# One gate/up block of a SwiGLU layer computed by Strassen's scheme in the Winograd form

## The chip, the cores and the metric

The kernel runs on one NeuronCore of a Trainium2 chip, alone. The metric is the device time of one execution in microseconds (us); lower is better. A core has five instruction streams: TensorE (PE; its weight loads are shown apart as PEld), VectorE (DVE), ScalarE (ACT), GpSimd (POOL) and SyncE (SP), the last used here only to issue DMAs. PE writes to PSUM, eight banks of 2 KB a partition; all else lives in SBUF.

## The reference, cut to what matters

The kernel computes one layer of a hybrid decoder for 256 tokens, all in float32. The change lies in the last two steps.

```python
D_MODEL = 1024; SEQ = 256
D_FF = -(-8 * D_MODEL // (3 * 256)) * 256          # 2816

def layer(x, ...):
    h = rms_norm(x, ln1_g)
    x = x + (sigmoid(g_a) * attention(h) + sigmoid(g_b) * ssm(h)) @ w_out
    h2 = rms_norm(x, ln2_g)
    x = x + (silu(h2 @ w_gate) * (h2 @ w_up)) @ w_down
    h3 = rms_norm(x, ln3_g)
    return x + (p @ w_ple_proj) * sigmoid(h3 @ w_ple_gate)
```

## The kernel before

**Splitting float32.** TensorE multiplies at its fast rate in a rounded format, so each float32 operand `a` is kept as `ah` (rounded) and `al = a - ah`, and each product takes three matmuls, `ah*wh + ah*wl + al*wh`, that add up in one PSUM bank. Activations are split once; weights on their way in. A weight tile is 128 rows x 2 k-tiles x 512 columns (512 KB). SP issues its load to `raw` (4 buffers), ACT rounds it to `wh` (5 buffers), and DVE subtracts to get `wl` (5 buffers): `split_w`, whose subtraction is L377 and whose rounding goes through the helper `act` at L254. Every matmul goes through the helper `mm` at L275.

**Panels.** A `Panel` is 256 tokens x 512 output columns in two PSUM banks (tiles named g), one for each half of the tokens. Its inner dimension of 1024 is eight k-tiles; `next_chunk()` gives four of them (two weight tiles), and a half panel is the 24 matmuls of 128x512 that these four feed: 4 k-tiles x 3 x 2 token halves.

**SwiGLU.** The 2816 columns of gate and of up are taken as five blocks of 512 and one of 256. A block is a gate panel and an up panel, four half panels or 96 matmuls. `Gated.gate` computes silu for each token half: ACT takes Sigmoid of the bank scaled by the row's `rstd2`, and DVE multiplies it by the scaled bank (L1509). `Gated.up` multiplies by the up bank (L1518), a DVE transpose turns 32x32 squares (L1527), and `send` moves the 16 pieces of 32 KB to their place with 16 DMAs issued on SP's queue (L1537). `split`, a task that waits until its due time, rounds the moved rows on ACT and subtracts on DVE (L1549); they are the operands of the down-projection, whose two panels of 22 k-tiles follow the gate/up blocks. Then `Residual` adds (L1432) and normalises, and `final` (L1600 to L1605) applies the last gate.

**What sets the order.** Each engine runs its own instructions in the order in which they were issued when the kernel was built, and waits on semaphores for the others. The order is made in the builder: `fill.spawn` registers a task, a generator that yields the model time at which it is due; `fill.step()` after each k-tile advances that time, and due tasks are issued there. `LAG`, and numbers such as 26000.0 in `split`, are such due times in model nanoseconds. `prio` ranks instructions for the scheduler, and `follow` holds one behind another. So a number in a table decides where in an engine's stream an instruction stands, and the hardware then takes it in that place.

Of the kernel before, what the change touches and what calls it, by code (L numbers as in the profile page):

```python
# [13 lines left out]
ALU = mybir.AluOpType  # L14
# [48 lines left out]
]  # L63
NFF = 11

NORMED = 5


def by_rows():
# [63 lines left out]
    "m": [11900, 6200],  # L133
    "res": [5337, 5987],
    "m.moved": [11625, 22875],
    "r.moved": [15000],
}
# [52 lines left out]
def tile_layer(ctx: ExitStack, tc: tile.TileContext, head, xk, pt, vec, w_dt, w_big, w_dn2, w_pp, out):  # L190
# [170 lines left out]

    def w_tiles():
        return (sb.tile([P, 2, 512], F32, tag="raw", bufs=RAW, name=nm("raw")),
                sb.tile([P, 2, 512], F32R, tag="wh", bufs=WH, name=nm("wh")),
                sb.tile([P, 2, 512], F32R, tag="wl", bufs=WL, name=nm("wl")))

# [1052 lines left out]
    class Residual:  # L1419
# [7 lines left out]
        def take(self, n, pan):  # L1427
# [51 lines left out]
    for n in range(2):  # L1479
# [15 lines left out]
    ff = []  # L1495

    class Gated:

        def __init__(self, w):
            self.w, self.f = w, []  # L1500

        def gate(self, pan, c):

            with prio("ev"):
                for tt, ps in enumerate(pan.ps):
                    r = rstd2[:, tt : tt + 1]
                    f = s2([self.w])
                    act(f, ps[:, c], AF.Sigmoid, scale=r)
                    stt(f, ps[:, c], r, f, op0=ALU.mult, op1=ALU.mult)  # L1509
                    self.f.append(f)  # L1510
# [20 lines left out]
        def send(self, turned):  # L1531
            n = self.both.shape[3]
            moved = s4([4, 2 * n])
            with prio("ev"):
                for a in range(4):
                    for b in range(4):
                        nc.sync.dma_start(  # L1537
                            moved[32 * b : 32 * b + 32, a], self.both[32 * a : 32 * a + 32, b].rearrange("p t n -> p (t n)"))
            fill.spawn(self.split(moved.rearrange("p a (x j) -> p x a j", j=32)), 0)

        def split(self, moved):

            yield fill.now + (26000.0 if self.w > 256 else 26500.0)
            n = self.w // P
            with prio("ev"):
# [25 lines left out]
    gated = Gated(512)  # L1571
    gated.gate(pans[0], WHOLE)
    gated.up(pans[1], WHOLE)
    for n in range(1, NFF // 2):
        gated = Gated(512)
        gated.gate(pans[2] if n == 1 else whole(), WHOLE)
        gated.up(whole(), WHOLE)
    pan = Panel()
    for k in (0, 4):
        pan.add(next_chunk(), h2[k : k + 4], last=k == 4)  # L1580
    gated = Gated(256)
    gated.gate(pan, HALVES[0])
    gated.up(pan, HALVES[1])

    res3 = Residual(xin, V_G3, rstd3, False)
    for n in range(2):
        pan = Panel()
        for c in range(4):
            ch = next_chunk()
            fill.drain(lambda: len(ff) >= 4 * c + 4)  # L1590
            pan.add(ch, ff[4 * c : 4 * c + 4], last=False)
        ch = next_chunk() + load(w_dn2[n], 2)
        fill.drain(lambda: len(ff) == 22)
# [16 lines left out]
def _layout(i):  # L1610
# [79 lines left out]
```

## Time and profile before

| | |
|---|---|
| three runs | 574.41, 575.56, 576.28 us; median 575.56 |
| the profiled execution | 574.76 us |
| its span, first to last instruction | 572.8 us |
| granted TensorE clock | 1.00 throughout |
| gate/up and down-projection | about 310 to 553 us of the span |
| GpSimd busy | 88.0 us (15%) |

Times come from the profile of one execution. "Busy" is the time in which an engine ran an instruction; groups of instructions are given by source line, engine, operation and shape, with the mean duration of one; "idle before" is the time in which the engine waited ahead of them, with what ended it. The chain that ended last is followed back from the last instruction; where it stays on one engine, that engine was never waiting. Rows on which the argument rests stand with the prediction.

### The profile page before, as it was taken

To read this page: it belongs to the slowest core of one execution; us is meant where nothing else is said; L and a number is where in the kernel's file an instruction comes from. 1 tells how busy PE (TensorE), PEld (TensorE's weight loads), DVE (VectorE), ACT (ScalarE), POOL (GpSimd) and SP (SyncE) were. 2 spreads that over 40 slices of the span, in tenths; PEclk is the share of its full clock that TensorE was granted. 3 is DMA by queue.
4 is the path that set the end of the run, shared out by engine and by line. 5 is a ranking of instruction groups with operands and counts; after the bars stand their busy time and mean duration, and the time that the engine had idled before them with its cause. 6 is when DMAs were issued, how large, how long until landed. Compare 5 with 4: busy or idle time off the path is not lost.

```text
span 572.8 us, 8553 instructions
## 1 busy us (share of the span) xinstructions
PE 567.3 (99%) x2971; PEld 476.0 (83%) x2971; DVE 444.5 (78%) x702; ACT 339.7 (59%) x532; POOL 88.0 (15%) x127
## 2 busy tenths in 40 slices
PE   9999999999999999999999999999999999999996
PEld 8887898988888888888887888888888888888885
DVE  6678899989999988898695976766767767556565
ACT  6855567676779579748574454646355445444452
POOL 2011223000533403211320200300000000002020
PEclk9999999999999999999999999999999999999999
DMA  8875698656476756757655785575677666657652
GB/s 317 325 265 175 222 266 238 208 153 180 156 191 185 208 177 173 257 162 249 186 168 190 267 287 194 167 273 184 197 238 242 210 214 233 219 190 256 196 173 73
DMA packets 43802, 121.22 MB, mean 212 GB/s; under 512 B 6384, under 2 KB 14608, under 8 KB 43760
## 3 DMA queue, kind: packets, MB, share of 16 engines
q1 hardware_dynamic: 39040, 107.71, 57.0%
q0 software_dynamic: 4144, 12.32, 8.6%
q10 hardware_dynamic: 576, 0.66, 0.4%
q8 instruction: 23, 0.38, 0.3%
q14 instruction: 19, 0.16, 0.1%
HBM read 111.28 MB, written 6.44 MB: 205 GB/s over the span
## 4 chain that ended last, share of the span: by engine, by line
PE 98%; DMA 1%; DVE 0%; ACT 0%; issue 0%
PE g L275 88%; PE pb L275 8%; PE pb L297 2%; DMA raw<-in_head 1%; ACT s L254 0%; DVE s L1603 0%; DVE s L1604 0%; DVE wh L373 0%
## 5 line engine op out<-in xcount | busy, mean ns | idle before, releaser
L275 PE MATMUL g<-wh,s 128*128 128x512 f32 (+1 forms) x1220 | 381.8, 390 | 0.1
L254 ACT ACTIVATE wh<-raw 128x1024 fp32r<-128x1024 f32 (+2 forms) x192 | 198.9, 1039 | 159.5 <-PE g L275 125.0
L377 DVE TENSOR_TENSOR wl<-raw,wh 128x1024 fp32r<-128x1024 f32 (+2 forms) x188 | 223.6, 1194 | 81.4 <-ACT wh L254 73.3
L275 PEld LDWEIGHTS g<-wh,s 128*128 128x128 f32 x1220 | 228.7, 189 | 47.5 <-issue 0.5
L275 PE MATMUL g<-wl,s 128*128 128x512 f32 (+1 forms) x610 | 235.6, 388 | 0.0
L275 PEld LDWEIGHTS g<-wl,s 128*128 128x128 f32 x610 | 114.6, 188 | 23.2 <-issue 0.4
L275 PE MATMUL g<-s,wh 128*128 128x512 f32 (+1 forms) x320 | 90.3, 353 | 0.0
L275 PE MATMUL g<-s,wl 128*128 128x256 f32 x256 | 69.2, 283 | 0.0
L275 PEld LDWEIGHTS g<-s,wh 128*128 128x128 f32 x320 | 54.8, 190 | 6.8 <-DVE s L1392 0.3
L275 PEld LDWEIGHTS g<-s,wl 128*128 128x128 f32 x256 | 48.5, 189 | 2.0 <-issue 0.2
L254 ACT ACTIVATE s<-s 128x512 f32<-128x512 f32 (+4 forms) x45 | 34.9, 786 | 17.6 <-DVE s L1432 5.6
L749 POOL DMA_DIRECT2D turn_d<-s x16 | 12.6, 788 | 194.9 <-DVE s L739 194.5
L275 PEld LDWEIGHTS pb<-s,s 128*64 128x64 f32 (+2 forms) x336 | 23.9, 158 | 5.8 <-issue 2.4
L275 PE MATMUL pb<-s,s 128*64 128x128 f32 (+5 forms) x336 | 28.7, 294 | 0.0
L254 ACT ACTIVATE s<-pb 128x512 f32<-128x512 f32 (+3 forms) x45 | 20.3, 481 | 13.7 <-PE pb L275 8.4
L254 ACT ACTIVATE s<-s,vecs 128x256 f32<-128x256 f32 (+1 forms) x48 | 23.3, 536 | 6.3 <-DMA s<-turn_d 5.3
L653 DVE SCALAR_TENSOR_TENSOR s<-s,vecs,s 128x255 f32<-128x255 f32 (+2 forms) x60 | 26.4, 478 | 0.0
L759 POOL DMA_DIRECT2D s<-turn_d x40 | 22.5, 595 | 25.3 <-DMA turn_d<-s 10.3
L886 POOL TENSOR_SCALAR_AFFINE_SELECT rr<-a_h 128x512 fp32r<-128x512 f32 x16 | 16.8, 1134 | 37.9 <-PE pb L275 21.6
L254 ACT ACTIVATE s<-s,tiny 128x128 f32<-128x128 f32 (+1 forms) x44 | 18.7, 444 | 5.9 <-DVE tiny L1086 5.9
L254 ACT ACTIVATE s<-g 128x256 f32<-128x256 f32 (+1 forms) x44 | 20.0, 472 | 1.3 <-PE g L275 1.3
L794 POOL TENSOR_TENSOR tiny<-tiny,mhalf 128x8 f32<-128x8 f32 x8 | 13.2, 1649 | 42.0 <-DVE tiny L792 41.6
(153 smaller groups left out, 382.0 us busy)
## 6 DMA issues: line engine op xcount, KB each, us to landing
raw<-in_w_big SPq DMA_DIRECT2D x176, 512.0 KB
turn_d<-s POOLq DMA_DIRECT2D x14, 256.0 KB, 4.7
s<-turn_d POOLq DMA_DIRECT2D x28, 128.0 KB, 4.9
wl<-in_w_big POOLq DMA_DIRECT2D x5, 512.0 KB, 8.0
s<-s SPq DMA_DIRECT2D x80, 32.0 KB
raw<-in_head SPq DMA_DIRECT2D x4, 512.0 KB
s<-in_xk SPq DMA_DIRECT2D x4, 512.0 KB
raw<-in_head SPq DMA_DIRECT2D x6, 256.0 KB
```

What stands on the lines that cost most here:

```text
L254: return nc.scalar.activation(o, i, f, **kw)
L275: ins = nc.tensor.matmul(o, lhsT, rhs, start=start, stop=stop).ins
L297: queue(nc.tensor.transpose(o, i, ident[: i.shape[0], : i.shape[0]]).ins, main)
L377: low = nc.vector.tensor_sub(wl, raw, wh.bitcast(F32))
L653: stt(cc[j][:, sft:], pu[:, j, : T - sft], cw[j][3 - sft], cc[j][:, sft:], op0=ALU.mult, op1=ALU.add)
L749: nc.gpsimd.dma_start(d[:, :, at : at + t_.shape[2]].rearrange("b p n -> p b n"), t_)
L759: by[via[b % len(via)]].dma_start(o[32 * b : 32 * b + 32], d[b].rearrange("(a i) n -> i a n", i=32))
L794: nc.gpsimd.tensor_tensor(f, ms, mhalf, op=ALU.pow)
L886: nc.gpsimd.affine_select(r, bcast(a_h[:, c, h0 : h0 + 4].bitcast(F32), P), pattern=[[0, 4], [1, P]], compare_op=ALU.is_ge, fill=0.0, base ...
```

## The change

The fourth of the five 512 blocks (`wino_block()` is 3, columns 1536 to 2047 of gate and of up) is computed as a product of 2x2 block matrices: the two token halves are the rows, the two halves of the inner dimension the middle, and gate and up the columns. Winograd's form of Strassen's scheme needs seven block products in place of eight. Each has 12 matmuls of 128x512 (4 k-tiles x 3) and a PSUM bank of its own (tiles named pb), so that the block takes 84 matmuls.

- **Weight sums.** `b11`, `b21` are gate's two K halves, `b12`, `b22` up's. A chain `q` in two SBUF tiles holds b11 for P1, has b12 added for P5, b22 for P6 and b21 for P4; a chain `r` holds b22 for P3 and has b12 added for P7; P2 takes b21 as it is. Each product has two tiles of 512 KB loaded and splits them as any other weight tile: 14 tiles where the block had 8. Of the eight additions of 128x1024, six are on VectorE and the two of P4 on GpSimd.
- **Activation sums.** `wino_rows` builds them on GpSimd from the split rows (one token half rescaled by the ratio of the two `rstd2`, which one more float32 matmul, `pr`, spreads over the partitions), and splits three of them with ACT and DVE.
- **Order.** `whole()` calls `gw.step()` ahead of the half panels numbered 1, 2, 4, 5, 6, 7 and 8 (`WINO_AT`), so one product runs before each: P1, P2, P5, P3, P6, P7, P4. The other blocks keep their order.
- **SiLU.** ACT computes Silu in one instruction; DVE's multiplication at L1509 is gone. In `final`, Sigmoid becomes Tanh of half the argument; `hrstd3` is that half, and `pj` is halved when it is evicted.
- **Moves.** The 16 DMAs of each block are issued from GpSimd's queue, four at a time in steps of `GAP`, and no longer from SP's. The due times of `split` and two rows of `LAG` are set anew.

```diff
+GAP = 1049
+WINO_AT = (1, 2, 4, 5, 6, 7, 8)
+SUMS = {('P2', 0), ('P3', 0), ('P3', 1), ('P5', 0), ('P5', 1), ('P6', 0), ('P6', 1), ('P7', 0), ('P7', 1)}
+ROWS = [18485, 28895, 2039, 6021, 1453, 0]
+SPLIT_AT = [58803, 53214]
...
-    "res": [5337, 5987],
+    "res": [4481, 1462],
...
-    "r.moved": [15000],
+    "r.moved": [19998],
...
+                        if not self.normed:
+                            nc.gpsimd.tensor_scalar(hrstd3[:, tt : tt + 1], self.dst[:, tt : tt + 1], 0.5, None, op0=ALU.mult)
...
-                copy = nc.vector.tensor_copy(pj[n][:, tt], pan.ps[tt])
+                copy = nc.vector.tensor_scalar(pj[n][:, tt], pan.ps[tt], 0.5, None, op0=ALU.mult)
...
+    def wino_rows():
+        yield fill.now + ROWS[0]
...
+        with prio("bg"):
...
+            pr = pb([P])
+            mm(pr, ones, rd, True, True)
+            prs = s2([P])
+            act(prs, pr)
+            a1, a2 = s4([2, 4, P]), s4([2, 4, P])
+            for h in range(2):
+                for k in range(4):
+                    hi, lo = (x.bitcast(F32) for x in res2.acts[h][k][:2])
+                    ptt(a2[:, h, k], hi[:, P:], lo[:, P:], op=ALU.add)
+                ptt(a2[:, h], a2[:, h], prs.unsqueeze(1).to_broadcast([P, 4, P]), op=ALU.mult)
...
+            ptt(a1[:, 0], a2[:, 0], a1[:, 0], op=ALU.subtract)
+            ptt(q, a1[:, 0], a2[:, 1], op=ALU.subtract)
+            ptt(a2[:, 0], a2[:, 0], a2[:, 1], op=ALU.subtract)
+            ptt(a1[:, 1], a1[:, 1], q, op=ALU.add)
+        for n, (a, ps) in enumerate(((a2, ("P5", "P4")), (a1, ("P7", "P3")), (q, ("P6",)))):
+            yield fill.now + ROWS[2 + n]
...
+                follow(act(h, a).ins, fill.cast)
+                nc.vector.tensor_sub(l, a, h.bitcast(F32))
...
+    class Wino:
+        TAKES = {"P1": ("q", "b11"), "P5": ("q", "b12"), "P6": ("q", "b22"), "P4": ("q", "b21"),
+                 "P3": ("r", "b22"), "P7": ("r", "b12"), "P2": (None, "b21")}
...
+                        if (chain, i) not in self.held:
+                            self.held[chain, i] = s4([2, 512])
+                            nc.sync.dma_start(self.held[chain, i], src)
+                        else:
+                            more = sb.tile([P, 2, 512], F32, tag="raw", bufs=RAW, name=nm("raw"))
+                            nc.sync.dma_start(more, src)
+                            on = nc.vector if (p, i) in SUMS else nc.gpsimd
+                            on.tensor_tensor(self.held[chain, i], self.held[chain, i], more, op=ALU.add)
+                        tiles = (self.held[chain, i], *w_tiles(1))
+                    fill.cast = split_w(tiles).ins
...
+        def product(self, p, ps=None, begin=True, end=True):
+            parts = self.load(p)
+            fill.drain(lambda: len(self.acts.get(p, ())) == len(parts))
...
+            for k, ((wh, wl), (ah, al)) in enumerate(zip(parts, self.acts[p])):
+                with prio("mm"):
+                    mm(ps, ah, wh, begin and k == 0, False, main=True)
+                    mm(ps, ah, wl, False, False, main=True)
+                    mm(ps, al, wh, False, end and k == len(parts) - 1, main=True)
+                fill.step()
...
-                    act(f, ps[:, c], AF.Sigmoid, scale=r)
-                    stt(f, ps[:, c], r, f, op0=ALU.mult, op1=ALU.mult)
+                    act(f, ps[:, c], AF.Silu, scale=r)
...
+        def moves(self, both):
+            n = both.shape[3]
             moved = s4([4, 2 * n])
-            with prio("ev"):
-                for a in range(4):
+            for a in range(4):
+                with prio("ev"):
                     for b in range(4):
-                        nc.sync.dma_start(
-                            moved[32 * b : 32 * b + 32, a], self.both[32 * a : 32 * a + 32, b].rearrange("p t n -> p (t n)"))
+                        follow(nc.gpsimd.dma_start(
+                            moved[32 * b : 32 * b + 32, a], both[32 * a : 32 * a + 32, b].rearrange("p t n -> p (t n)")).ins, fill.last)
+                yield fill.now + GAP
...
-            yield fill.now + (26000.0 if self.w > 256 else 26500.0)
+            yield fill.now + SPLIT_AT[self.w == 256] - 4 * GAP
...
+    class GatedWino(Gated):
...
+            p1 = product("P1")
+                act(v1, p1, scale=r)
+            p2 = product("P2")
+                stt(c11, p2, r, v1, op0=ALU.mult, op1=ALU.add)
+                act(f1, c11, AF.Silu)
+            p5 = product("P5")
+            p3 = product("P3")
+            p6 = product("P6")
+                stt(v1, p6, r, v1, op0=ALU.mult, op1=ALU.add)
+                stt(c12, p5, r, v1, op0=ALU.mult, op1=ALU.subtract)
+                stt(c12, p3, r, c12, op0=ALU.mult, op1=ALU.add)
+                nc.vector.tensor_mul(f1, f1, c12)
+            p7 = product("P7")
+                stt(v1, p7, r, v1, op0=ALU.mult, op1=ALU.subtract)
+                stt(c22, p5, r, v1, op0=ALU.mult, op1=ALU.add)
+                turned = [self.turn(f1, 0)]
+            p4 = product("P4")
+                stt(v1, p4, r, v1, op0=ALU.mult, op1=ALU.subtract)
+                act(f2, v1, AF.Silu)
+                nc.vector.tensor_mul(f2, f2, c22)
+                self.send(turned + [self.turn(f2, 1)])
...
     def whole():
         pan = Panel()
         for k in (0, 4):
+            if half_no[0] in WINO_AT:
+                gw.step()
+            half_no[0] += 1
             pan.add(next_chunk(), h2[k : k + 4], last=k == 4)
...
-                act(t, ps, AF.Sigmoid, scale=rstd3[:, tt : tt + 1])
-                nc.vector.tensor_mul(t, t, pj[n][:, tt, c])
+                act(t, ps, AF.Tanh, scale=hrstd3[:, tt : tt + 1])
+                stt(t, t, 1.0, pj[n][:, tt, c], op0=ALU.add, op1=ALU.mult)
```

What this moves on the engines is shown at three places. A row is a source line, an operation, the tile written and the tiles read, with the tiles' numbers, and how often it repeats. The new file's helpers stand some ten lines lower: L286 is `mm`, L387 the subtraction of `split_w`, L1625 a weight sum, L1664 the multiplication by up, L1673 the transpose, L1687 a move, L1735 to L1753 the evictions of products.

The first place is TensorE at the end of the first half panel that `whole()` makes. Before, one half panel (s4_814 is the last activation k-tile of it) is followed by the other:

```order
L275 MATMUL g_846_4250<-wh_851_4258,s4_814_4043 128x512 x2
L275 MATMUL g_846_4250<-wl_852_4259,s4_814_4043 128x512
L275 MATMUL g_846_4250<-wh_851_4258,s4_814_4043 128x512
L275 MATMUL g_845_4249<-wh_854_4288,s4_791_3948 128x512
L275 MATMUL g_845_4249<-wl_855_4289,s4_791_3948 128x512
```

Now:

```order
L286 MATMUL g_851_4258<-wh_856_4266,s4_820_4076 128x512
L286 MATMUL pb_865_4324<-wh_860_4314,s4_819_4066 128x512
L286 MATMUL pb_865_4324<-wl_861_4315,s4_819_4066 128x512
L286 MATMUL pb_865_4324<-wh_860_4314,s4_819_4066 128x512 x2
L286 MATMUL pb_865_4324<-wl_861_4315,s4_819_4066 128x512
L286 MATMUL pb_865_4324<-wh_860_4314,s4_819_4066 128x512
L286 MATMUL pb_865_4324<-wh_863_4320,s4_820_4076 128x512
L286 MATMUL pb_865_4324<-wl_864_4321,s4_820_4076 128x512
L286 MATMUL pb_865_4324<-wh_863_4320,s4_820_4076 128x512 x2
L286 MATMUL pb_865_4324<-wl_864_4321,s4_820_4076 128x512
L286 MATMUL pb_865_4324<-wh_863_4320,s4_820_4076 128x512
L286 MATMUL g_850_4257<-wh_870_4342,s4_791_3948 128x512
```

P1, on two weight tiles that serve one token half only (6 matmuls for each tile, where a half panel has 12), stands between the half panels.

The second place is VectorE, from the first half panel's splits of a block to its last. Before, in the block of the same place, splits (L377) alternate with the block's own work:

```order
L377 TENSOR_TENSOR wl_967_4889<-raw_965_4887,wh_966_4888 128x1024
L1509 SCALAR_TENSOR_TENSOR s2_946_4786<-g_930_4706,rstd2_3712,s2_946_4786 128x512
L377 TENSOR_TENSOR wl_970_4895<-raw_968_4893,wh_969_4894 128x1024
L377 TENSOR_TENSOR wl_973_4925<-raw_971_4923,wh_972_4924 128x1024
L1518 SCALAR_TENSOR_TENSOR s2_945_4783<-g_947_4789,rstd2_3712,s2_945_4783 128x512
L1527 STREAM_TRANSPOSE s4_961_4864<-s2_945_4783 128x4x4x32
L377 TENSOR_TENSOR wl_976_4931<-raw_974_4929,wh_975_4930 128x1024
```

Now, from the sums for P7 (s4_922 and s4_925 are chain r) to the splits of half panel no. 7 (wl_964, wl_967):

```order
L1625 TENSOR_TENSOR s4_922_4586<-s4_922_4586,raw_953_4739 128x1024
L387 TENSOR_TENSOR wl_949_4697<-raw_947_4695,wh_948_4696 128x1024
L1625 TENSOR_TENSOR s4_925_4592<-s4_925_4592,raw_956_4746 128x1024
L1664 SCALAR_TENSOR_TENSOR s2_903_4511<-g_905_4515,rstd2_3712,s2_903_4511 128x512
L387 TENSOR_TENSOR wl_952_4703<-raw_950_4701,wh_951_4702 128x1024
...
L387 TENSOR_TENSOR wl_958_4750<-s4_925_4592,wh_957_4749 128x1024
L1735 SCALAR_TENSOR_TENSOR s2_866_4337<-pb_944_4668,rstd2_3712,s2_866_4337 128x512
L387 TENSOR_TENSOR wl_964_4773<-raw_962_4771,wh_963_4772 128x1024
L1737 SCALAR_TENSOR_TENSOR s2_946_4691<-pb_913_4531,rstd2_3712,s2_866_4337 128x512
L387 TENSOR_TENSOR wl_967_4779<-raw_965_4777,wh_966_4778 128x1024
L1738 SCALAR_TENSOR_TENSOR s2_946_4691<-pb_928_4598,rstd2_3712,s2_946_4691 128x512
L387 TENSOR_TENSOR wl_974_4817<-s4_859_4312,wh_973_4816 128x1024
```

The sums stand ahead of splits that an earlier matmul needs, and an eviction of a product stands between any two splits.

The third place is GpSimd, whose queue holds nothing in this part of the kernel before. Before, between the first norm's end and the second's:

```order
L759 DMA s4_772_3871<-turn_d_761_3843 32x4x256 x4
L1450 TENSOR_TENSOR tiny_777_3908<-ss_734_3714 128x1
L518 TENSOR_SCALAR tiny_778_3910<-tiny_777_3908 128x1
L519 TENSOR_TENSOR rstd2_3712<-tiny_778_3910,mhalf_80 128x1
L749 DMA turn_d_1035_5227<-s2_1033_5223 128x4x128
```

Now, from the end of the activation sums on:

```order
L1531 TENSOR_TENSOR s4_838_4159<-s4_838_4159,s2_836_4156 128x512 x2
L1542 TENSOR_TENSOR s4_837_4158<-s4_838_4159,s4_837_4158 128x512
L1543 TENSOR_TENSOR rr_892_4452<-s4_837_4158,s4_838_4159 128x512
L1544 TENSOR_TENSOR s4_838_4159<-s4_838_4159 128x512
L1545 TENSOR_TENSOR s4_837_4158<-s4_837_4158,rr_892_4452 128x512
L1687 DMA s4_858_4274<-s4_847_4249 32x256 x16
L1687 DMA s4_885_4400<-s4_875_4378 32x256 x16
L1625 TENSOR_TENSOR s4_859_4312<-s4_859_4312,raw_972_4813 128x1024
L1625 TENSOR_TENSOR s4_862_4318<-s4_862_4318,raw_975_4820 128x1024
L1687 DMA s4_945_4672<-s4_935_4648 32x256 x16
L1687 DMA s4_986_4860<-s4_961_4769 32x256 x16
```

The moves of all blocks but the first two stand behind P4's two sums, which wait for the loads of raw_972 and raw_975.

More of the change, by code (lines that the diff above doesn't have):

```diff
@@ L64, with wino_block @@
 NFF = 11
+GAP = 1049
[3 more added lines that the diff above has]
+SPLIT_AT = [58803, 53214]
+def wino_block():
+    return 1 + sum(WINO_AT[-1] > half for half in (1, 5, 9))
 NORMED = 5
@@ L360, in tile_layer, with w_tiles @@
     chunk_no = [0]
[L362 to L365, printed above, removed]
+    def w_tiles(first_=0):
+        return [sb.tile([P, 2, 512], dt, tag=tag, bufs=bufs, name=nm(tag))
+                for tag, dt, bufs in (("raw", F32, RAW), ("wh", F32R, WH), ("wl", F32R, WL))[first_:]]
     def split_w(tiles, js=slice(0, 2), c=WHOLE, on=None):
@@ new lines, in blocks_of, with wino_acts, tiles, take @@
+    def blocks_of(t):
+        return t.rearrange("p n (a j) -> p n a j", a=4)
+    def wino_acts(a11, a12, a21, a22, ops, rank, own=("P1", "P2", "P4")):
+        n = a11.shape[1]
+        two = n == 2
+        def tiles(dt):
+            if two:
+                t = s4([4, n, P], dt)
+                return [t], [t[:, i] for i in range(4)]
+            ts = [s4([2, n, P], dt) for _ in range(2)]
+            return ts, [t[:, i] for t in ts for i in range(2)]
+        def take(p, hi, lo):
+            ops.setdefault(p, []).extend((hi[:, k], lo[:, k]) for k in range(n))
+        def plain(p, a, new):
+            o = new([2, n, P], F32R)
+            follow(act(blocks_of(o[:, 0]), a).ins, fill.cast)
+            nc.vector.tensor_sub(blocks_of(o[:, 1]), a, blocks_of(o[:, 0].bitcast(F32)))
+            take(p, o[:, 0], o[:, 1])
+        with prio(rank):
+            whole32, (q, s4_, s1, m3) = tiles(F32)
+            vtt = nc.vector.tensor_tensor
+            vtt(blocks_of(m3), a21, a11, op=ALU.subtract)
+            vtt(blocks_of(q), blocks_of(m3), a22, op=ALU.subtract)
+            vtt(blocks_of(s4_), a12, blocks_of(q), op=ALU.add)
+            vtt(blocks_of(s1), a21, a22, op=ALU.subtract)
+            for p, a in (("P1", a11), ("P2", a12), ("P4", a22)):
+                if p in own:
+                    plain(p, a, s2 if two else s4)
+            his, hi = tiles(F32R)
+            los, lo = tiles(F32R)
+            for w, h, l in zip(whole32, his, los):
+                follow(act(h, w).ins, fill.cast)
+                nc.vector.tensor_sub(l, w, h.bitcast(F32))
+            for i, p in enumerate(("P6", "P3", "P5", "P7")):
+                take(p, hi[i], lo[i])
@@ new lines, in tile_layer, with __init__, load @@
+    class Wino:
+        TAKES = {"P1": ("q", "b11"), "P5": ("q", "b12"), "P6": ("q", "b22"), "P4": ("q", "b21"),
+                 "P3": ("r", "b22"), "P7": ("r", "b12"), "P2": (None, "b21")}
+        def __init__(self, acts, srcs):
+            self.acts, self.srcs, self.held = acts, srcs, {}
+        def load(self, p):
+            chain, b = self.TAKES[p]
+            parts = []
+            with prio("w"):
+                for i, src in enumerate(self.srcs[b]):
+                    if chain is None:
+                        tiles = w_tiles()
+                        nc.sync.dma_start(tiles[0], src)
+                    else:
+                        if (chain, i) not in self.held:
+                            self.held[chain, i] = s4([2, 512])
+                            nc.sync.dma_start(self.held[chain, i], src)
+                        else:
+                            more = sb.tile([P, 2, 512], F32, tag="raw", bufs=RAW, name=nm("raw"))
[4 more added lines that the diff above has]
+                    fill.cast = split_w(tiles).ins
+                    parts += parts_of(tiles)
+            return parts
+        def product(self, p, ps=None, begin=True, end=True):
+            parts = self.load(p)
+            fill.drain(lambda: len(self.acts.get(p, ())) == len(parts))
+            if ps is None:
+                ps = pb([512])
+            for k, ((wh, wl), (ah, al)) in enumerate(zip(parts, self.acts[p])):
[4 more added lines that the diff above has]
+                fill.step()
+            return ps
@@ L1562, in tile_layer, with wino_srcs @@
     h2 = res2.acts[0] + res2.acts[1]
+    def wino_srcs():
+        srcs = {}
+        for b in ("b11", "b21", "b12", "b22"):
+            src = next_src()
+            srcs[b] = [src[:, k : k + 2] for k in (0, 2)]
+        return GatedWino(srcs)
+    gated = Gated(512, 0)
+    gated.gate(pans[0], WHOLE)
+    gated.up(pans[1], WHOLE)
+    half_no = [0]
     def whole():
@@ L1567, in whole @@
         for k in (0, 4):
+            if half_no[0] in WINO_AT:
+                gw.step()
+            half_no[0] += 1
             pan.add(next_chunk(), h2[k : k + 4], last=k == 4)
         return pan
[L1571 to L1575, printed above, removed]
+    gw = wino_srcs()
+    for n in range(1, NFF // 2 - 1):
+        gated = Gated(512, n + (n >= wino_block()))
         gated.gate(pans[2] if n == 1 else whole(), WHOLE)
         gated.up(whole(), WHOLE)
[L1578 to L1581, printed above, removed]
+    pan = whole()
+    gated = Gated(256, NFF // 2)
     gated.gate(pan, HALVES[0])
@@ L1585, in tile_layer @@
     res3 = Residual(xin, V_G3, rstd3, False)
+    hrstd3 = const.tile([P, 2], F32, name="hrstd3")
     for n in range(2):
```

66 lines of the change are left out of this document (58 added, 8 removed).

## The prediction

> **What bounds the kernel now.** I read the page first: the span, the busy shares, and the chain that ended last by engine.
>
> ```profile
> span 572.8 us, 8553 instructions
> PE 567.3 (99%) x2971; PEld 476.0 (83%) x2971; DVE 444.5 (78%) x702; ACT 339.7 (59%) x532; POOL 88.0 (15%) x127
> PE 98%; DMA 1%; DVE 0%; ACT 0%; issue 0%
> ```
>
> TensorE is the bound, so time falls where matmuls go and the others keep up. Where the change lies, two views show how tight this is: a long piece of the chain, and the busy times of three windows (PE, PEld, DVE, ACT, POOL, then granted clock, DMA share, GB/s).
>
> ```profile
> 396.54 157.11 PE g L275 x696
> 400.00:550.00 150.00, 150.00 (x663) 124.23 (x662) 100.38 (x109) 73.45 (x83) 5.67 (x9) 1.00 0.68 219
> 371.00:382.00 11.00, 11.00 (x50) 9.13 (x49) 8.76 (x15) 5.41 (x6) 0.00 (x0) 1.00 0.84 289
> 10.00:20.00 10.00, 10.00 (x46) 8.29 (x45) 8.46 (x14) 7.62 (x12) 0.00 (x0) 1.00 1.03 384
> ```
>
> PE doesn't pause for 150 us, at full clock: no wait is left here for the change to remove. One matmul of 128x512 takes 157.11/696 = 0.2257 us, a half panel (24) 5.42, a product (12) 2.71. DVE works 100 of 150 us, ACT 73, GpSimd hardly. What follows PE how closely, the waits of 400 to 550 us say (engine, line, releaser: us, times, longest):
>
> ```profile
> ACT wh L254 <- PE g L275: 57.6, 46, 3.3
> DVE wl L377 <- ACT wh L254: 28.5, 28, 1.8
> ```
>
> ACT mostly waits for PE to give back a wh buffer, and DVE for ACT. The weight pipeline thus runs as far ahead as five buffers let it: tile n is rounded once PE is done with tile n-5.
>
> **The change on TensorE.** Twelve matmuls fewer: 12 x 0.2257 = 2.71 us. One float32 matmul of 128x128, pr, is new:
>
> ```profile
> L309 PE MATMUL pb<-const-float32-0.0 128*128 128x128 f32 x14 | 3.3, 430 | 0.8 <-PEq L1679 0.8
> L275 PE MATMUL pb<-s,s 128*128 128x128 f32 x40 | 5.8, 277 | 0.0
> ```
>
> The first row is of float32 constants, each matmul in two records: 3.3/7 = 0.47 us. The second, 5.8/40 = 0.145 a record, gives 0.29 for two. I take 0.47, the row of the same type. Net 2.71 - 0.47 = 2.24 (2.42 at the lower price). Each matmul has its own weight load before and after (2971 of both), so a product's matmul has no reason to cost more than a panel's. All else costs time only if TensorE comes to wait.
>
> **VectorE in the stretch.** The densest part is from P5 through P4: five products and four half panels, 60 + 96 = 156 matmuls, 35.2 us. It takes two weight tiles each, 18 in all, one per 1.96 us, where a half panel alone takes one per 2.71. The rows for its work, from 340 to 553 us:
>
> ```profile
> L377 DVE TENSOR_TENSOR wl<-raw,wh 128x1024 fp32r<-128x1024 f32 x78 | 94.8, 1221 | 50.5 <-ACT wh L254 43.2 <-DMA s<-s 4.4 <-DMA raw<-in_w_dn 1.5
> L254 ACT ACTIVATE wh<-raw 128x1024 fp32r<-128x1024 f32 x78 | 82.4, 1061 | 84.7 <-PE g L275 69.2 <-issue 4.7 <-DMA raw<-in_w_big 3.9
> L1509 DVE SCALAR_TENSOR_TENSOR s<-g,rstd,s 128x512 f32<-128x512 f32 x10 | 7.5, 745 | 4.5 <-ACT s L254 4.5
> L1518 DVE SCALAR_TENSOR_TENSOR s<-g,rstd,s 128x512 f32<-128x512 f32 x8 | 6.0, 747 | 1.5 <-PE g L275 1.5
> L1527 DVE STREAM_TRANSPOSE s<-s 128x512 f32<-128x512 f32 x10 | 7.1, 706 | 0.1
> L254 ACT ACTIVATE s<-g,rstd 128x512 f32<-128x512 f32 x10 | 6.8, 681 | 5.3 <-PE g L275 5.3
> ```
>
> The ten instructions at 0.745 us (7.5 us) leave VectorE, though not at this place, where at most two would have stood. In program order, from the sums for P5 to the last split for P4, stand 18 splits and 6 sums of 128x1024 at 1.221 (a sum has the split's shape and two inputs: the same price), 2.5 splits of activation sums (3.1), five evictions at 0.745 (3.7), two transposes (1.4), and one multiplication (0.7): 38.2 us. The work is due between 0 us and 33.9 us (P4's second tile) of the stretch, so it must begin before it and never fall behind. Back to back it goes faster:
>
> ```profile
> 368.80 3.48 DVE L377 TENSOR_TENSOR wl<-raw,wh 128x1024 fp32r<-128x1024 f32 x3
> ```
>
> Three took 3.48, 1.16 each: 36.3 us for the whole. VectorE is full either way, and what counts is the lead over PE at each split. I count from the start of the first half panel of `whole()` with PE never waiting: P5 starts at 27.1, P3 at 35.2, half panel 5 at 37.9, P6 at 43.3, half panel 6 at 46.0, P7 at 51.5, half panel 7 at 54.2 (its second tile 56.9), P4 at 59.6 (61.0), half panel 8 at 62.3. P6's second split (wl_943) can't end before 38.8: its buffer is free at 36.55, when P3's first tile is done, plus 1.06 and 1.22. From there by single durations: sum 40.1, wl_949 41.3, sum 42.5, the eviction of half panel 5's result waits for it until 43.3 and ends at 44.1, wl_952 45.3, transpose and eviction 46.7, wl_955 48.0, transpose 48.7, wl_958 49.9, eviction 50.6, wl_964 51.8, needed at 54.2. The tightest lead is **2.4 us**, and the next, wl_967 at 53.8 for 56.9, is 3.1.
>
> **Loads.** SP issues in order and raw has four buffers. raw_953, the operand of the first of those sums, stands behind raw_950, whose buffer is free after the split wl_934, at 35.6. So three loads are issued there at once. The first load of the kernel shows what one takes with nothing ahead:
>
> ```profile
> 0.79 2.94 DMA raw<-in_head
> ```
>
> 2.94 us; the next tiles follow at 524 KB by the rate, 1.37 us at the 384 GB/s of 10 to 20 us, 1.81 at the 289 of 371 to 382. raw_953 lands at 39.9 to 40.4, up to 1.6 us after 38.8; the wait for half panel 5 takes in 1.0 of it, and the lead falls to 1.7 to 2.1. In all, 18 tiles and about 1 MB of moves in 35.2 us are 297 GB/s, between the two. At the 219 of 150 us (2.4 a tile) the same walk still leaves 1.2 us, so loads alone don't stop PE. The 96 moves that leave SP's queue and come to GpSimd's:
>
> ```profile
> L1537 SPq DMA_DIRECT2D s<-s x96: 507/588/597, 401.8 to 504.6; - x96
> L759 POOL DMA_DIRECT2D s<-turn_d x40: 551/556/912, 73.4 to 529.8; - x40
> ```
>
> 16 x 0.588 = 9.4 us of each block's issue go from SP, which helps loads, and 16 x 0.556 = 8.9 us come to GpSimd, which has nothing else to do. After its last matmul at 84.0 the 256 block has until 105.7, when the down-projection's fifth group (96 matmuls later) needs it: 3 for evictions, 8.9 issue, 3 landing, 2.3 split make 101; at 0.912 a move it would be 107, 1 us late. I take nothing.
>
> **GpSimd.** It is off the path except for P4's two sums, and no addition of this size is in the trace. The nearest row is the mask, with one input of half the size:
>
> ```profile
> L886 POOL TENSOR_SCALAR_AFFINE_SELECT rr<-a_h x16: 624/974/3708, 89.4 to 224.1; 128x512 fp32r<-128x512 f32 x16
> 187.46 4.48 POOL L886 TENSOR_SCALAR_AFFINE_SELECT rr<-a_h 128x512 fp32r<-128x512 f32 x2 [0.89 <-PE pb L275]
> 188.85 1.21 DVE L377 TENSOR_TENSOR wl<-raw,wh 128x1024 fp32r<-128x1024 f32 x1
> 191.37 1.11 DVE L951 TENSOR_TENSOR s<-s,s 128x512 f32<-128x512 f32 x1
> 90.18 2.03 DVE L611 TENSOR_TENSOR a_l<-tiny_dt,a_h 128x64 fp32r<-128x64 f32 x1
> 89.37 2.75 POOL L886 TENSOR_SCALAR_AFFINE_SELECT rr<-a_h 128x512 fp32r<-128x512 f32 x4
> ```
>
> Free, 0.624, or 1.25 at twice the size; two inputs up to double, 2.5. I take 2.3, near the end for two inputs. Beside VectorE additions a mask took up to 3.7 and VectorE's 128x64 subtraction 2.03, so one engine holds the other up, mostly GpSimd the loser: at 188.85 a split took its usual 1.21.
>
> raw_972 and raw_975 are issued with raw_965 after wl_952 (45.5 to 46.0) and land at about 50.3 and 51.9. GpSimd adds from 50.3 to 52.6 and to 54.9; the rounding and split of P4's second tile are through at 57.2 for 61.0. Without interference there is no stall. If a sum of s us holds VectorE for its whole length, once before wl_964 (52.1) and once before wl_967, the latter ends at 52.1 + s + 1.97 + s against 56.9: a stall of 2s - 2.8, at 2.3 **1.8 us**. The ends are 0 and 1.8; since the rows have GpSimd lose more often than VectorE I take less than half, 0.7.
>
> [...]
>
> The 22 activation sums are 5120 columns, 5 x 2.3 = 11.5 us, before P5 and in pieces of 0.3 and 1.2 us, each within a lead of five tiles; VectorE's 50.5 us of idle time cover them. ACT's nine more roundings (9.5 us) have 76 free. Silu I price as Sigmoid, 0.681: four stand in a row ahead of P1's rounding, 2.7 us, with 5.4 until P1. Tanh and the halved pj replace operations of the same shape.
>
> **Sum.** 574.76 - 2.24 = 572.5 for the profiled execution, whose time outside the span (2.0) stays; it lies 0.80 below the median of the runs, so 573.3, and with 0.7 given back **574.0**.
>
> **Rivals.**
> - *No stall* (573.3, down to 572.0 by a price of 0.29 for pr and a run as low as the fastest shown, 1.1 under the median). For it: the walk's 1.7 us of lead, and 1.16 instead of 1.22 a split. Against it: VectorE is full over 35 us.
> - *The lock at its dearest*, ending slower. P4's sums at the contended 3.7 each, in front of wl_964 and wl_967: 2 x 3.7 - 2.8 = 4.6, so 577.9. It is slower by 0.3% from a stall of 4.0, that is from s = 3.4. For it: the one row of 3.7, of half the columns. Against it: VectorE's own rows there hardly grow, and loads that land a little later put the second sum behind wl_967.
> - *The matmuls saved bring nothing*, or the last moves are late: 574.76 + 0.80 + 0.47 = 576.0 without any saving, 574.3 with the moves 1 us late. Against it: PE's unbroken 150 us, and the issue prices above.
>
> **How the numbers follow.** Short stall of 0.2 to 1.8 us: 0.40 (574.0, range 573.5 to 575.1). No stall: 0.30. The dearest lock: 0.17 (577.3 to 579). The rest, 575.1 to 577.3: 0.13. A measurement of this kernel tells about 0.3%, 1.7 us, from no change, so faster ends at 573.8 and slower begins at 577.3. Faster gets the 0.30 and 0.06 of the short stall, slower 0.17 and 0.02, the same 0.45. The range is 572.0 to 578.0.
>
> **What would show it.** In the changed profile, the chain between P5 and P4 stays on PE if there is no stall; a short one shows as idle time of PE before half panel 7 or P4, ended by DVE's splits. The sums on GpSimd show their price beside 2.3, and VectorE's splits beside them more than 1.3 us if the lock decides. The total of PE's matmuls in number must be twelve less. I am wrong if PE waits for a load in the stretch, if P1 is late behind the four Silus, or if the down-projection waits for the last moves.

## The result and the profile after

The changed kernel took 579.39 us (median of seven runs, 577.03 to 581.48) against 575.56: the ratio is 1.0063, 95% interval 1.0047 to 1.0079. It is slower, above the range of the forecast. The profiled run is its slowest, 581.48 us. One run told of below, 585.06 us of the kernel called "both", was in a slower state and is left out of its median. The page of the profiled run, the lines of the span, the busy shares, the granted clock in 40 slices and the chain by engine:

```profile
span 579.3 us, 8621 instructions
PE 569.6 (98%) x2961; PEld 474.4 (82%) x2961; DVE 461.9 (80%) x715; ACT 347.7 (60%) x543; POOL 164.9 (28%) x249
PEclk9999999999999999999999999999999899999999
PE 77%; DVE 10%; DMA 6%; issue 3%; POOL 2%; ACT 2%; SPq 0%; ACTq 0%; DVEq 0%
```

TensorE has ten records fewer (twelve matmuls less, and pr's two), and yet the chain leaves it: VectorE and DMA hold 16% of it, before 1%. What PE waited for (us, times, longest), and the four places in its timeline, with the idle time and its releaser in brackets:

```profile
PE g L286 <- DVE wl L387: 3.8, 4, 1.9
440.07 0.50 PE L286 MATMUL g<-wl,s 128*128 128x512 f32 x1 [0.62 <-DVE wl L387]
447.76 0.50 PE L286 MATMUL g<-wl,s 128*128 128x512 f32 x1 [0.60 <-DVE wl L387]
458.32 0.50 PE L286 MATMUL g<-wl,s 128*128 128x512 f32 x1 [1.86 <-DVE wl L387]
461.63 0.80 PE L286 MATMUL g<-wl,s 128*128 128x512 f32 x1 [0.73 <-DVE wl L387]
```

P5 starts at 426.60, so the prediction's clock starts at 399.5. The four stalls lie at the second tile of half panel 5, at the start of half panels 6 and 7, and at the second tile of 7, all ended by VectorE's splits. The same stretch by windows (columns as in the prediction):

```profile
425.00:435.00 10.00, 10.00 (x46) 8.27 (x45) 6.34 (x7) 5.44 (x8) 2.99 (x7) 1.00 0.95 321
435.00:445.00 10.00, 9.38 (x41) 7.19 (x40) 7.29 (x7) 5.36 (x6) 0.00 (x0) 1.00 0.62 201
445.00:455.00 10.00, 9.40 (x41) 7.14 (x40) 9.65 (x11) 4.24 (x4) 0.19 (x1) 1.00 0.64 220
455.00:465.00 10.00, 7.41 (x21) 5.09 (x20) 10.00 (x8) 3.75 (x4) 9.37 (x10) 0.69 0.60 180
```

VectorE, meant to be full, is idle for 3.7 us in the first window and 2.7 in the second, and full when it is too late. In the last window the granted clock is 0.69: 3.1 us of TensorE's time are lost to the clock there in this run, behind the longest stall. The loss does not hang on the clock: three of the seven runs have a mean clock of 0.993 or 0.994 (581.48, 579.55 and 580.27 us), the other four of 0.998 to 1.000, and these took 577.03 to 579.39. Where VectorE's time went shows its timeline, with SP's issue of P3's weights and GpSimd's sums:

```profile
422.35 1.03 SPq L1620 DMA_DIRECT2D s<-in_w_big  x2
432.72 1.23 DVE L387 TENSOR_TENSOR wl<-s,wh 128x1024 fp32r<-128x1024 f32 x1 [3.37 <-ACT wh L265]
439.93 2.35 DVE L387 TENSOR_TENSOR wl<-s,wh 128x1024 fp32r<-128x1024 f32 x2
445.35 1.23 DVE L1625 TENSOR_TENSOR s<-s,raw 128x1024 f32<-128x1024 f32 x1 [3.06 <-DMA raw<-in_w_big]
454.81 5.68 POOL L1625 TENSOR_TENSOR s<-s,raw 128x1024 f32<-128x1024 f32 x2 [24.45 <-DVE wl L387]
455.33 2.94 DVE L387 TENSOR_TENSOR wl<-raw,wh 128x1024 fp32r<-128x1024 f32 x1
458.85 2.73 DVE L387 TENSOR_TENSOR wl<-raw,wh 128x1024 fp32r<-128x1024 f32 x1
```

and the chain in the same place, in order of time:

```profile
419.67 2.28 DVE s L1625 x2
...
422.35 9.18 DMA s<-in_w_big
431.63 1.06 ACT wh L265
...
438.91 6.42 DMA raw<-in_w_big
...
447.62 1.22 DVE s L1625
```

P5's sums (419.67) give back two raw buffers; only then does SP get past the loads that wait for these, and issue P3's weights (422.35), which need no raw buffer at all. They land 9.2 us later, while the DMA engines are at 0.95 with the loads issued just before and the moves. VectorE stands 3.4 us at P3's split and 3.1 us at P7's first sum. wl_943 ends at 442.3, where the prediction had 438.3 as the earliest. Then GpSimd's sums meet wl_964 and wl_967, which take 2.94 and 2.73 us in place of 1.22.

### The profile page after: what moved, and what is told of

Same layout as the page of the kernel before. It is cut to its first block, busy times and chain, and to the rows that moved or that the text cites. A ratio compares the mean times of both kernels' runs of the same rounds, so it can differ in the third digit from the quotient of the medians.

```text
span 579.3 us, 8621 instructions
## 1 busy us (share of the span) xinstructions
PE 569.6 (98%) x2961; PEld 474.4 (82%) x2961; DVE 461.9 (80%) x715; ACT 347.7 (60%) x543; POOL 164.9 (28%) x249
## 4 chain that ended last, share of the span: by engine, by line
PE 77%; DVE 10%; DMA 6%; issue 3%; POOL 2%; ACT 2%; SPq 0%; ACTq 0%; DVEq 0%
PE g L286 66%; PE pb L286 9%; DVE wl L387 4%; DMA raw<-in_w_big 2%; PE pb L308 2%; POOL tiny L804 2%; DMA s<-in_w_big 2%; DVE s L663 1%; DVE s L1625 1%; ACT wh L265 1%; DMA s<-turn_d 1%; DMA turn_d<-s 1%; DMA raw<-in_head 1%; DVE s L1369 1%; ACT s L265 1%
## 5 line engine op out<-in xcount | busy, mean ns | idle before, releaser
L286 PE MATMUL g<-wh,s 128*128 128x512 f32 (+1 forms) x1156 | 365.1, 392 | 0.7 <-ACT s L265 0.7
L265 ACT ACTIVATE wh<-raw 128x1024 fp32r<-128x1024 f32 (+2 forms) x186 | 191.6, 1038 | 133.2 <-PE g L286 90.7
L387 DVE TENSOR_TENSOR wl<-raw,wh 128x1024 fp32r<-128x1024 f32 (+2 forms) x182 | 220.8, 1219 | 59.9 <-ACT wh L265 58.5
L286 PEld LDWEIGHTS g<-wh,s 128*128 128x128 f32 x1156 | 217.3, 189 | 46.5 <-ACT s L265 1.1
L286 PE MATMUL g<-wl,s 128*128 128x512 f32 (+1 forms) x578 | 224.9, 391 | 3.8 <-DVE wl L387 3.8
L286 PEld LDWEIGHTS g<-wl,s 128*128 128x128 f32 x578 | 109.0, 189 | 28.9 <-DVE wl L387 6.9
L286 PE MATMUL g<-s,wh 128*128 128x512 f32 (+1 forms) x320 | 90.5, 353 | 0.1
L286 PE MATMUL g<-s,wl 128*128 128x256 f32 x256 | 69.2, 283 | 0.0
L286 PEld LDWEIGHTS g<-s,wh 128*128 128x128 f32 x320 | 54.7, 189 | 7.3 <-DVE s L1402 0.5
L1687 POOL DMA_DIRECT2D s<-s x96 | 47.2, 498 | 30.2 <-issue 12.8
L265 ACT ACTIVATE s<-s 128x512 f32<-128x512 f32 (+4 forms) x49 | 38.2, 789 | 22.1 <-DVE s L1442 5.2
L286 PEld LDWEIGHTS g<-s,wl 128*128 128x128 f32 x256 | 48.4, 189 | 2.0 <-issue 0.2
L286 PE MATMUL pb<-wh,s 128*128 128x512 f32 (+1 forms) x96 | 29.9, 372 | 0.0
L759 POOL DMA_DIRECT2D turn_d<-s x16 | 12.6, 789 | 59.2 <-DVE s L749 59.2
L286 PE MATMUL pb<-s,s 128*64 128x128 f32 (+5 forms) x336 | 28.7, 294 | 0.0
L286 PEld LDWEIGHTS pb<-s,s 128*64 128x64 f32 (+2 forms) x336 | 23.9, 158 | 5.8 <-issue 2.4
L804 POOL TENSOR_TENSOR tiny<-tiny,mhalf 128x8 f32<-128x8 f32 x8 | 15.9, 1985 | 41.1 <-DVE tiny L802 41.1
```

The costliest lines, as they stand in the source:

```text
L265: return nc.scalar.activation(o, i, f, **kw)
L286: ins = nc.tensor.matmul(o, lhsT, rhs, start=start, stop=stop).ins
L387: low = nc.vector.tensor_sub(wl, raw, wh.bitcast(F32))
L759: nc.gpsimd.dma_start(d[:, :, at : at + t_.shape[2]].rearrange("b p n -> p b n"), t_)
L804: nc.gpsimd.tensor_tensor(f, ms, mhalf, op=ALU.pow)
L1687: follow(nc.gpsimd.dma_start(moved[32 * b : 32 * b + 32, a], both[32 * a : 32 * a + 32, b].rearrange("p t n -> p (t n)")).ins, fill.last)
```

## The experiments

Sixteen kernels ran. Before, run again beside them, took 575.24 to 575.56. The expectations weigh explanations by letter: A, P3's weights land late; B, the lock: each of GpSimd's additions holds VectorE up for its whole length; C, the other edits cost the time; D, the ring of four raw buffers goes round late; E, the DMA engines can't carry the traffic; F, VectorE has too much to do; G, VectorE's sums and late loads use up its lead, and only then do GpSimd's additions stop TensorE. Medians and ratios to before:

| kernel | us | ratio, 95% interval |
|---|---|---|
| changed kernel | 579.39 | 1.0063 (1.0047 to 1.0079) |
| products undone, other edits kept | 575.19 | 0.9997 (0.9988 to 1.0006) |
| no sums | 572.0 | 0.9941 (0.9929 to 0.9954) |
| all sums by DMA | 572.83 | 0.9968 (0.9944 to 0.9991) |
| P4's sums left out | 574.82 | 0.9991 (0.9975 to 1.0006) |
| P4's sums on VectorE | 577.6 | 1.0041 (1.0026 to 1.0056) |
| chain r loaded early | 577.32 | 1.0044 (1.0028 to 1.0059) |
| six raw buffers | 576.29 | 1.0017 (1.0002 to 1.0032) |
| six raw, P4 on VectorE | 576.53 | 1.0018 (1.0003 to 1.0034) |
| P4 by DMA | 575.63 | 1.0006 (0.9990 to 1.0023) |
| P4 by DMA, r early | 575.53 | 1.0001 (0.9985 to 1.0017) |
| P4 by DMA, six raw | 575.92 | 1.0002 (0.9986 to 1.0019) |
| six unread additions on VectorE | 575.35 | 1.0007 (0.9987 to 1.0028) |
| two unread additions on GpSimd | 574.0 | 0.9984 (0.9964 to 1.0004) |
| both | 579.05 | 1.0065 (1.0038 to 1.0092) |
| all by DMA, moves on SP | 585.46 | 1.0183 (1.0160 to 1.0206) |
| P4 on GpSimd, rest by DMA, moves on SP | 587.49 | 1.0215 (1.0195 to 1.0235) |

**What the matmuls and the other edits are worth.** Without `gw.step()` and `wino_rows` (products undone):

> The block is computed as before, in 96 matmuls without products and sums; Silu, Tanh, the moves from GpSimd's queue and the due times stay as changed. Theories A and B: 575.0 to 576.0, the time of before, since TensorE had no wait for them to remove. Theory C (moves behind GpSimd, four Silus in a row, due times): 577 or more.

575.19. Silu, Tanh, the moves and the due times cost nothing: theory C falls. With every product on its plain block:

```diff
-                    if chain is None:
+                    if True:
```

> Leaves out all eight weight sums: every product takes its block of weights as loaded, so the number of loads, splits and matmuls stays and no addition is made by either engine. Theories A and B both: PE never waits in the stretch, 573.3 (572.5 to 574.0), the price of the matmuls alone. Theory C: 576 or more, since all other edits are still there.

572.0, below the 573.3 expected. A part is the price of pr: in the changed kernel's chain stand

```profile
385.69 2.98 PE pb L286 x14
394.12 2.72 PE pb L286 x12
```

a product with pr's two records and one without, so that pr costs 0.26 us and not 0.47. The matmuls are worth 2.71 - 0.26 = 2.45 us; the 3.4 us measured here have an interval of 2.6 to 4.1, so about 0.2 at the least is not accounted for.

**The two suspects by themselves.** P4's sums moved to VectorE (`SUMS` with P4), and chain r's first loads issued at P5:

> P4's two weight sums are added by VectorE, so that GpSimd adds nothing in the stretch. Theory A (loads: the in-order load queue lets P3's weights land late, VectorE idles 3.4 us and its lead is gone from then on): the two sums of 1.22 us take the place of the 3.2 us by which GpSimd stretched two splits, little changes, 578 to 579.5. Theory B (lock: the two stretched splits are what stops PE): the long stall before half panel 7 goes and the lowered clock with it, 575 to 576. Theory C (the other edits cost the time): 579.4.

> The first loads of chain r (P3's weights, buffers of their own) are issued at P5, ahead of the raw loads that wait for P5's sums; nothing else changes. Theory A: P3's weights land before 426 us of the span in place of 431.5, VectorE's idle 3.4 us before P3's splits goes, the two stalls of 0.6 us go, the third shrinks: 574 to 576. Theory B: VectorE is stretched by GpSimd before half panel 7 all the same and PE stops there for 1.5 to 2 us: 577.5 to 578.5. Theory C: 579.4.

577.6 and 577.32: each takes away about 2 us, hardly more than the spread of the runs, of the 6.6 between the changed kernel and the sums by DMA below, neither alone the whole. The first is in no theory's range, the second 0.2 below that of B. With r early PE stops only twice, but longer (2.24 and 1.66 us, VectorE stretched to 3.35 and 2.73). P4's sums left out altogether (`if p == "P4"`: plain tiles):

> Leaves out P4's two weight sums alone (P4 takes its block as loaded); VectorE's order up to P4's splits, the loads and the ring of four stay. Theory B: GpSimd adds nothing, the long stall goes, 573 to 574.5. Theory D: the ring still goes round late, the stall before half panel 7 stays at 1 to 2 us or more, 576 to 577.5.

574.82, 4.6 us less than the changed kernel and 0.3 above what theory B gave; the stalls of half panel 7 are gone, those in 5 and before 6 stay. So the two additions on GpSimd cost 4.6 us in their place, on VectorE 2.8 (577.6).

**Another way to add.** The chain's tile is accumulated by DMA:

```diff
-                            more = sb.tile([P, 2, 512], F32, tag="raw", bufs=RAW, name=nm("raw"))
-                            nc.sync.dma_start(more, src)
-                            on = nc.vector if (p, i) in SUMS else nc.gpsimd
-                            on.tensor_tensor(self.held[chain, i], self.held[chain, i], more, op=ALU.add)
+                            nc.gpsimd.dma_start(self.held[chain, i], src, accum_op=ALU.add)
```

> All eight sums are made by the DMA itself: the block is accumulated from HBM into the chain's tile by a DMA on GpSimd's queue, so a sum takes no raw buffer, no instruction of VectorE or GpSimd. Theory D (the ring of four raw buffers: loads for sums are given back late, in VectorE's order, so that four loads go round in about 10 us where TensorE uses four tiles in 8.1): no stall, 572 to 573.5, faster than before. Theory B (lock): the same. Theory E (the extra 3 MB are what the DMA engines can't carry): stalls stay, 577 or more.

572.83, as expected, and faster than both kernels. Its window from 400 to 475 us:

```profile
400.00:475.00 75.00, 75.00 (x332) 61.96 (x331) 60.79 (x63) 45.32 (x48) 35.42 (x67) 1.00 0.90 258
```

TensorE never waits, with the DMA engines at 0.90. Two of the twelve runs took 577.35 and 578.93 us; the trace is of another, and what held them up is open. With the moves back on SP's queue, first with all eight sums by DMA, then with P4's two on GpSimd:

> All eight sums by accumulating DMAs, the moves issued from SP's queue as before the change. Theory G: 572.3 to 573.3, TensorE without a wait in the stretch; the moves' queue makes no difference. If the moves on GpSimd's queue delay the accumulation now and then (two runs of twelve took 577 to 579 there): the same median without such runs.

> Six sums by accumulating DMAs, P4's two on GpSimd as in the changed kernel, the moves back on SP's queue; VectorE's order is that of the run with all sums by DMA and moves on SP, so the two differ by GpSimd's additions alone. Theory G (VectorE's six sums and the late loads use up the lead, and only then do GpSimd's additions stop TensorE): VectorE's splits beside them still take 2.7 to 3.3 us, but PE doesn't wait, 572.5 to 573.7. Theory B (the lock alone stops PE): 575 or more.

585.46 and 587.49: the moves back on SP's queue, which were meant as a detail, cost 12.6 us. SP's timeline in the first of the two shows a part of why:

```profile
398.66 1.05 SPq L1620 DMA_DIRECT2D s<-in_w_big  x2
399.75 7.94 SPq L1684 DMA_DIRECT2D s<-s  x11
408.11 1.12 SPq L405 DMA_DIRECT2D raw<-in_w_big  x1
```

Eleven moves hold the weight loads back for 8 us, and VectorE's and ScalarE's splits end TensorE's waits at 405 to 442 us: it starts 302 matmuls from 400 to 475 us where it started 332. The rest comes later, in the down-projection, where the moved rows are late and TensorE waits 4.2 us for their rounding:

```profile
520.12 0.69 PE L286 MATMUL g<-wh,s 128*128 128x512 f32 x1 [3.53 <-ACT s L265]
```

So the products, at the changed kernel's due times, can't have these moves on SP's queue. The kernel before had them there without a wait of TensorE; whether the products or the due times make the difference was not tried. Between these two runs the lock can still be read from the trace: beside GpSimd's additions two splits take 2.81 and 2.76 us, and PE does not wait between 443 and 470 us. So GpSimd's additions did not stop it there, with VectorE ahead. The second median is 2.0 us above the first all the same, with intervals that meet; what the additions have to do with that is open.

**Ring of buffers, or VectorE's time.** Six raw buffers, alone and with P4's sums elsewhere:

> Six raw buffers instead of four, paid for by two of the 26 scratch buffers s4; sums and engines as in the changed kernel. Theory D: VectorE no longer waits 3 us for a load at P7's first sum, the two stalls of 0.6 us go and the one before half panel 7 shrinks from 1.9: 573.5 to 575.5. Theory B: the two splits beside GpSimd's sums still take 2.7 to 2.9 us and PE stops there: 577 to 578. Theory E: as the changed kernel.

> As the run with six raw buffers, and P4's two sums on VectorE. Theory D and B together: both causes are gone, 572.5 to 574. Theory F (VectorE simply has too much to do, 8 sums and 18 splits in 35 us): 576 or more.

> P4's two sums by accumulating DMAs, the other six on VectorE as in the changed kernel. Theory G: the long stall before half panel 7 is gone, the two shorter ones before half panels 5 and 6 stay: 574.3 to 575.3, as where P4's sums were left out. Theory E (the DMA accumulation is itself a cost): 576 or more.

> As the run before, and chain r's first loads issued at P5. Theory G with late loads as the cause of the two short stalls: 573.0 to 574.2. If the early issue only moves the wait to the next load: 574.5 to 575.3.

> P4's sums by accumulating DMAs, the other six on VectorE, six raw buffers and 24 scratch buffers. Theory D (ring of raw buffers and late loads): 572.8 to 574.3. Theory F (VectorE's time): no better than with four raw buffers, 575 to 576.

In this order they took 576.29, 576.53, 575.63, 575.53 and 575.92. The first lies between the ranges of D and B, the second and the last are as theory F had them, the two between are above what G gave. Six buffers help where GpSimd adds (3.1 us), with P4's sums on VectorE by 1.1, which the spread of the runs can hide, and not at all with P4 by DMA: the time is then 575.5 to 575.9 whatever the buffers or the loads of r. Theory D falls for what VectorE's six sums cost. The lock is shown by the first of these, in the timelines of VectorE and GpSimd:

```profile
446.43 0.71 DVE L1673 STREAM_TRANSPOSE s<-s 128x512 f32<-128x512 f32 x1
446.91 5.75 POOL L1625 TENSOR_TENSOR s<-s,raw 128x1024 f32<-128x1024 f32 x2 [11.64 <-DMA raw<-in_w_big]
447.06 3.33 DVE L387 TENSOR_TENSOR wl<-raw,wh 128x1024 fp32r<-128x1024 f32 x1
450.31 0.74 DVE L1664 SCALAR_TENSOR_TENSOR s<-g,rstd,s 128x512 f32<-128x512 f32 x1
450.97 2.77 DVE L387 TENSOR_TENSOR wl<-s,wh 128x1024 fp32r<-128x1024 f32 x1
L1625 POOL TENSOR_TENSOR s<-s,raw x2: 2396/2896/3395, 446.9 to 449.3; 128x1024 f32<-128x1024 f32 x2
```

The first addition takes 2.40 us, to 449.31; the split that began at 447.06 ends 1.08 later. The second addition waits for that split (3.40 us), and the next split waits for it (2.77). A multiplication with an operand in PSUM (0.74) passed at its usual price (0.747 before). So did a transpose, which has one input (0.71, before 0.706), as the changed kernel shows at an activation sum:

```profile
396.13 1.29 POOL L1545 TENSOR_TENSOR s<-s,rr 128x512 f32<-128x512 f32 x1
396.38 0.71 DVE L1673 STREAM_TRANSPOSE s<-s 128x512 f32<-128x512 f32 x1
```

Last, additions that are tied to no load and no raw buffer (operands long there, result unread; each does take a scratch buffer), beside sums by DMA. The first kernel has those on VectorE; the second asks for `p == "P4"` instead, and the third for both:

```diff
+                            if p != "P4":
+                                on = nc.vector if (p, i) in SUMS else nc.gpsimd
+                                on.tensor_tensor(s4([2, 512]), xin[0], xin[1], op=ALU.add)
```

> All sums by accumulating DMAs, and six further additions of 128x1024 on VectorE in the stretch whose operands have long been there and whose result nobody reads: VectorE's work is that of the changed kernel without its ties to loads and raw buffers. Theory F: 574.5 to 576, as with the true sums. Theory D: 572.5 to 573.5, since VectorE's work still fits and only the ties cost.

> All sums by accumulating DMAs, and two further additions of 128x1024 on GpSimd near P4's place, unread. Theory G (GpSimd's additions only hurt where VectorE has no lead): VectorE's splits beside them are stretched to 2.7 to 3.3 us, PE doesn't wait, 572.5 to 573.5. Theory B: 574.5 or more.

> Both: six unread additions on VectorE and two on GpSimd, all true sums by DMA. Theory F with the lock: 577 or more, about the changed kernel's time. Theory D with G: 573 to 574.5, so that the rest of the changed kernel's loss is due to the ties to loads and raw buffers.

575.35, 574.0 and 579.05, against 572.83 without. Six additions on VectorE cost 2.5 us, two on GpSimd 1.2, and both 6.2, about the changed kernel's time. The last kernel's runs spread from 575.66 to 582.84, so that its excess over the sum of 3.7 isn't sure by itself. The true sums bear it out: beside VectorE's six, GpSimd's two cost 3.8 (579.39 against 575.63 with P4 by DMA). Theory F holds for the size, and theory G is only half right: alone, GpSimd's additions cost 1.2 and not nothing. The second kernel's timelines show where:

```profile
460.17 6.03 DVE L387 TENSOR_TENSOR wl<-raw,wh 128x1024 fp32r<-128x1024 f32 x1
460.34 4.76 POOL L1625 TENSOR_TENSOR s<-s,s 128x1024 f32<-128x1024 f32 x2
466.26 0.50 PE L286 MATMUL g<-wl,s 128*128 128x512 f32 x1 [1.33 <-DVE wl L387]
```

By these times the split began 0.17 us before the first addition, and was held through both even so. The last kernel's show both waits of VectorE:

```profile
440.02 0.75 DVE L1664 SCALAR_TENSOR_TENSOR s<-g,rstd,s 128x512 f32<-128x512 f32 x1 [4.91 <-PE g L286]
460.87 4.75 POOL L1625 TENSOR_TENSOR s<-s,s 128x1024 f32<-128x1024 f32 x2
461.07 5.64 DVE L387 TENSOR_TENSOR wl<-raw,wh 128x1024 fp32r<-128x1024 f32 x1
```

Here too nothing stands between the two additions, and one split waits for both: 5.64 us for work of 1.22. And though no load holds VectorE, it stands 4.9 us at an eviction that its queue has ahead of the next splits. This is how we read that 36 us of work don't fit into 35: VectorE, in order, has waits there that it can't fill. From 415 to 465 us they are (engine, line, releaser: us, times, longest), in the changed kernel, then in this last one:

```profile
DVE wl L387 <- ACT wh L265: 4.9, 3, 3.4
DVE s L1625 <- DMA raw<-in_w_big: 3.1, 1, 3.1
```

```profile
DVE s L1664 <- PE g L286: 4.9, 1, 4.9
DVE wl L387 <- ACT wh L265: 2.6, 1, 2.6
```

8.0 and 7.5 us, from different causes. The same additions in another order, which would show that it is the waits, were not tried.

## Why the prediction was wrong

- **Matmuls.** Right: 12 fewer, 2.71 us. pr was mis-sized (0.26 for 0.47). The forecast without a stall, 573.3, is met by the sums by DMA, 572.83.
- **Silu, Tanh, activation sums, moves.** Right in that they cost nothing (575.19 without products and activation sums; 572.0 with activation sums and no weight sums). That the moves' queue matters was missed: 12.6 us hung on it beside sums by DMA.
- **VectorE in the stretch: the step that failed.** The amount of work was right (a sum took 1.218 us, as a split). The walk began at wl_943, "can't end before 38.8", and went on as if it ended then; it ended at 42.8. "VectorE is full either way" was false: it stood 3.4 us at P3's splits and 3.1 at P7's sum, so that the lead of 2.4 us was gone, with PE stopped in half panel 5, before GpSimd added anything.
- **Loads.** The prediction followed raw_953's place in SP's queue and not that of chain r's own tiles, one burst earlier. The two loads in the chain took 9.2 and 6.4 us there and not 2.9 and 1.4 to 1.8 for each next one. As a cause by itself this was worth about 2 us (577.32), and nothing once GpSimd's sums were gone.
- **GpSimd's sums.** The price was right: 2.37 and 2.40 us where they ran first, for 2.3; the longer ones, 3.35 and 3.40, hold a wait for a split. "I take less than half" of the lock was wrong: VectorE was held to the end of each addition; in the timeline of six raw buffers the two splits, work of 1.22 us each, end 1.08 us after an addition does (450.39 after 449.31, 453.74 after 452.66). The rows of the mask, read as GpSimd losing (a split beside one took 1.21), were of one input.
- **A deadline.** The stall by the lock was counted against a wrong time. The second half panel of a panel (5 and 7 here) takes all four k-tiles for one token half first (`add` with `last`), so its second tile is due after six matmuls and not after twelve: at 55.6 and not 56.9. In the trace the stalls at 440.07 and 461.63 come at the eighth matmul of half panels 5 and 7, the first that reads the second tile's wl. So by the same walk the tightest lead was wl_967's 1.8 us, and the stall 2s - 1.5, at 2.3 already 3.1 us in place of 1.8.
- **The rivals.** The slower one came nearest (577.9), by luck: its 4.6 us of stall stood for two sums of 3.7 each. Its decision point, a sum of 3.4 us, wasn't what decided: at 2.4 each, with the lead already gone, 4.6 us were lost. VectorE's time and GpSimd's lock were weighed as two cases, and they add to more than their sum: 2.5 and 1.2 alone, 6.2 together.
- **Not foreseen:** the lower clock behind a stall, in three of the seven runs by their mean clock (0.993 or 0.994).

## What to carry to other kernels

Before work is put on an engine that is close to full, walk its queue in order through the whole stretch and write down each wait, from the first load that starts it; the idle time of an in-order engine need not be room: here VectorE stood at waits for 8.0 us from 415 to 465 us, and TensorE waited 3.8 us for its splits all the same. Two costs that draw on one lead must be added before they are compared with it. A sum of streamed weights needs no instruction of VectorE or GpSimd that adds: a DMA that accumulates into the tile took bandwidth (the DMA engines were at 0.90 from 400 to 475 us) and 0.86 us of GpSimd's queue each, and both were there.

## What the runs showed of the hardware

The granted clock can fall behind a stall: in the changed kernel's profile it was 0.88 from 455 to 460 us and 0.50 from 460 to 465, behind a stall of 1.86 us; with chain r early, behind stalls of 2.24 and 1.66 us, it stayed at 1.00 in the profiled run, while three others of its twelve have a mean clock of 0.994. So the clock fell behind a stall of 1.86 us once, and another time not behind one of 2.24. What decides it is open.

The other fact is the time of the accumulating DMAs, from the view of DMA issues of the kernel with all sums by DMA, 400 to 475 us (line, queue, count, KB each, us from issue to landing):

```profile
s<-in_w_big POOLq DMA_DIRECT2D x8, 512.0 KB, 10.0
```

10.0 us at the median, where TensorE waited for none of them.
